# The MLP's down projection as seven block products: an fp32 decoder step on one Trainium2 core

## The chip, the cores and the metric

The kernel runs on one core of a Trainium2 chip. The metric is the device time of one execution in microseconds (us). TensorE is PE in the profile (its weight loads are PEld), VectorE is DVE, ScalarE is ACT, GpSimd is POOL and SyncE is SP. SP issues most of the transfers between HBM and SBUF here.

## The reference

The reference is one step of a two-layer decoder over 1056 tokens (1024 of a prompt and 32 of samples), width 1024, all in fp32. Each layer has a mixer (S5 and SSD scans in the first layer, sparse attention in the second) and then the MLP that this change is about:

```
D_MODEL = 1024;  D_FF = 4 * D_MODEL
rms_norm(x, g):  x * rsqrt(mean(x * x, -1) + 1e-5) * g
every layer:     x += relu(rms_norm(x) @ w_up)^2 @ w_down     # w_up 1024 x 4096, w_down 4096 x 1024
at the end:      y = rms_norm(x)
```

## The kernel before

**Three matmuls for a product.** TensorE takes its operands in the rounded fp32 form `fp32r`. To keep fp32's accuracy, each operand is split: hi is ACT's cast of it, lo is DVE's subtraction of hi from it. A product is hi·hi + hi·lo + lo·hi, three matmuls into the same PSUM bank (L384 to L386 in `dense`, L1355 to L1357 in the up projection). So every operand of TensorE costs one ACT and one DVE instruction first.

**The layout.** Activations lie with features on the 128 partitions and tokens along the free dimension. The 1056 tokens are two halves of `HF` = 528 in the MLP, each of two parts of 264.

**The up projection** (`mlp`, `prep`, `prod`) runs already as seven products of 2x2 blocks in place of eight: the weights and the normalised activations are each seen as 2x2 blocks, sums of blocks are formed, seven products p1 to p7 are made with matmuls of 264 columns, and the results are combined on the way out of PSUM (banks A, B and C). There are 16 passes `p`, each giving two of the 32 tiles of hidden features; the order of the products in a pass is p1, then p3 of the pass before, p6, p2, p7, p5, p4. `prep` makes the weights' sums on POOL (L1310) and splits them (L1321 and L1322). `act` makes relu² on DVE (L1337, a SCALAR_TENSOR_TENSOR), multiplies by `r2`, the squared norm factor of each token, on POOL (L1338), and SP writes the tile to the HBM buffer `h_d`.

**The down projection** (`h_load`, `down`, `dense`) is the plain product: 8 groups `G` of 512 hidden features x 8 output tiles `d` x 3 token chunks of 352 x 4 tiles `k` x 3 matmuls. For each group `h_load` reads four hidden tiles back from `h_d` and splits them (L330, L331); a unit of 512 KB of `w_dn` is loaded and split on ACT and DVE (L315, L316) with two buffers. DVE adds each finished bank into `Y` (L1400); at G = 6 the residual is added, at G = 7 `finish` squares `Y` and, after layer 0, makes the next layer's normalised operands `xn` (`resid`, L1192 and L1197).

**Order.** The program is written as one stream of Python; the tile framework gives every engine its own queue of instructions in program order, lifts work inside `tc.high_priority` (the weights' splits) ahead, and places the waits from tiles' buffers: a tile of a tag with n buffers waits until the nth tile before it was last read. `held` keeps the first two units of `w_dn` from being loaded before the up phase is nearly over. `W` carries the split activations of the up phase, `R` the raw weights, `SW` the split weights and `E` the partial results on their way out.

## Time and profile before

| | us |
|---|---|
| median of 3 runs | 3173.86 |
| lowest and highest | 3172.98, 3180.18 |
| the profiled execution | 3170.71 |
| its span in the trace | 3168.8 |
| PE busy | 3037.3 (96%) |
| DVE busy | 2081.9 (66%) |
| ACT busy | 1290.5 (41%) |
| POOL busy | 784.0 (25%) |

Busy times are those of instructions on an engine, and overlap with those of the others. The time outside the span (1.9 us in the profiled execution) is launch and end. A row of the timeline gives an instruction's start, its length and, in brackets, how long its engine was idle before and what released it; matmuls overlap in the array, so the distance from one start to the next, not the length, tells what a matmul costs.

### The profile page before, as it was taken

The numbers are of one execution on the slowest core, as the hardware profiler recorded it, in microseconds if no ns is written. First come the engines' busy times: TensorE is split into PE (matmuls) and PEld (weight loads), VectorE is DVE, ScalarE is ACT, GpSimd is POOL, SyncE is SP. The second block draws the span as 40 slices with busy tenths as digits, with TensorE's granted clock in tenths as the row PEclk, the third lists the DMA queues.
The fourth block names the chain that finished last, engine by engine and source line by source line (L and its number), as shares of the span: only waits on it lengthen the run. The fifth ranks groups of instructions, "written<-read, shape, count | busy, mean of one in ns | idle before, by whom it ended". The sixth has DMA issues, their size and how long they took to land. (4 is left out here: it accounts for less than half of the span.)

```text
span 3168.8 us, 55263 instructions
## 1 busy us (share of the span) xinstructions
PE 3037.3 (96%) x21451; PEld 2871.4 (91%) x21451; DVE 2081.9 (66%) x4075; ACT 1290.5 (41%) x2575; POOL 784.0 (25%) x771
## 2 busy tenths in 40 slices
PE   7999998998999999999999989999999999999998
PEld 5999886898999999999999777777778999999998
DVE  4778787788766444466224777878776776644456
ACT  4223666434333321123236666666653333331112
POOL 0000000016666200001001344343333666510000
PEclk8999999999999999999999999999999999999999
DMA  5345453522333532228631122121143233353232
GB/s 185 94 128 156 113 131 120 165 85 94 106 107 106 173 101 96 67 87 247 163 92 57 18 67 59 23 61 41 21 119 118 95 106 109 113 174 99 78 93 80
DMA packets 219852, 328.55 MB, mean 104 GB/s; under 512 B 71283, under 2 KB 164694, under 8 KB 219526
## 3 DMA queue, kind: packets, MB, share of 16 engines
q1 hardware_dynamic: 189760, 264.03, 27.5%
q0 software_dynamic: 17728, 36.77, 4.7%
q10 hardware_dynamic: 12102, 24.22, 2.0%
q8 instruction: 169, 2.77, 0.4%
q14 instruction: 93, 0.76, 0.1%
HBM read 224.30 MB, written 92.22 MB: 100 GB/s over the span
## 5 line engine op out<-in xcount | busy, mean ns | idle before, releaser
L384 PE MATMUL mm<-hh,wh 128*128 128x352 f32 x1440 | 465.1, 323 | 0.2 <-ACT c L1363 0.2
L386 PE MATMUL mm<-hh,wh 128*128 128x352 f32 x1440 | 464.9, 323 | 0.0
L385 PE MATMUL mm<-hh,wh 128*128 128x352 f32 x1440 | 464.5, 323 | 0.0
L1400 DVE TENSOR_TENSOR Y<-Y,mm 128x352 f32<-128x352 f32 x336 | 173.8, 519 | 273.1 <-PE mm L386 272.3
L315 ACT CAST wh<-wr 128x1024 fp32r<-128x1024 f32 (+3 forms) x121 | 122.9, 1016 | 468.8 <-PE mm L385 453.4
L1355 PE MATMUL A<-xw,sw 128*128 128x264 f32 x1024 | 291.7, 286 | 2.3 <-ACT xw L1215 1.6
L1357 PE MATMUL A<-xw,sw 128*128 128x264 f32 x1024 | 292.4, 286 | 1.0 <-DVE sw L1322 1.0
L1356 PE MATMUL A<-xw,sw 128*128 128x264 f32 x1024 | 293.0, 286 | 0.1
L2124 POOL TENSOR_SCALAR P<-P,s,gates 128x640 f32<-128x640 f32 (+7 forms) x256 | 211.9, 841 | 277.1 <-DVE s L2120 229.0
L385 PEld LDWEIGHTS mm<-hh,wh 128*128 128x128 f32 x1440 | 271.2, 188 | 0.0
L384 PEld LDWEIGHTS mm<-hh,wh 128*128 128x128 f32 x1440 | 270.7, 188 | 0.4 <-ACT c L1363 0.4
L386 PEld LDWEIGHTS mm<-hh,wh 128*128 128x128 f32 x1440 | 270.9, 188 | 0.0
L1338 POOL TENSOR_TENSOR e<-e,r 128x264 f32<-128x264 f32 x192 | 196.6, 1030 | 225.1 <-DVE e L1337 221.6
L384 PE MATMUL mm<-xh,wh 128*128 128x352 f32 x672 | 224.5, 335 | 7.0 <-ACT xh L435 5.9
L385 PE MATMUL mm<-xl,wh 128*128 128x352 f32 x672 | 222.5, 331 | 5.2 <-DVE xl L436 5.2
L386 PE MATMUL mm<-xh,wh 128*128 128x352 f32 x672 | 221.7, 330 | 0.0
L2142 DVE TENSOR_TENSOR PT<-px,PT 128x512 fp32r<-128x512 f32 x264 | 176.8, 682 | 51.2 <-ACT PT L2141 50.6
L316 DVE TENSOR_TENSOR wh<-wr,wh 128x1024 fp32r<-128x1024 f32 (+3 forms) x121 | 143.8, 1188 | 100.1 <-ACT wh L315 100.1
L2166 PE MATMUL pv<-PT,vs 128*128 128x512 f32 x528 | 195.3, 438 | 11.6 <-ACT PT L2141 6.8
L2116 ACT ACTIVATE P<-sc,m 128x640 f32<-128x640 f32 (+7 forms) x256 | 180.1, 713 | 41.0 <-DVE m L2110 30.1
L1355 PEld LDWEIGHTS A<-xw,sw 128*128 128x128 f32 x1024 | 193.8, 190 | 2.9 <-ACT xw L1215 1.7
L1357 PEld LDWEIGHTS A<-xw,sw 128*128 128x128 f32 x1024 | 194.1, 190 | 1.4 <-DVE sw L1322 1.4
(631 smaller groups left out, 8305.6 us busy)
## 6 DMA issues: line engine op xcount, KB each, us to landing
hr<-h_d SPq DMA_DIRECT2D x64, 528.0 KB
wu<-i_w_up SPq DMA_DIRECT2D x64, 512.0 KB
wr<-i_w_dn SPq DMA_DIRECT2D x64, 512.0 KB
h_d<-e SPq DMA_DIRECT2D x192, 132.0 KB
wr<-i_w_in_e POOLq DMA_DIRECT2D x26, 512.0 KB, 4.1
h_d<-c SPq DMA_DIRECT2D x64, 132.0 KB
res<-res SPq DMA_DIRECT2D x48, 176.0 KB
csb<-cs_d SPq DMA_DIRECT2D x16, 512.0 KB
```

The costliest lines, as they stand in the source:

```text
L384: T.matmul(o, wh, xh, start=(j == 0), stop=False)
L385: T.matmul(o, wh, xl, start=False, stop=False)
L386: T.matmul(o, wl, xh, start=False, stop=(j == n - 1))
L1338: nc.gpsimd.tensor_tensor(x, x, st["r2"][:, tok], OP.mult)
L1355: T.matmul(o, a, xh, start=bool(first and q == 0), stop=False, skip_group_check=True)
L1356: T.matmul(o, a, xl, start=False, stop=False, skip_group_check=True)
L1357: T.matmul(o, b, xh, start=False, stop=(q == 3), skip_group_check=True)
L1400: V.tensor_tensor(y[:, cc], y[:, cc], p[:, :CH], OP.add)
L2116: S.activation(P, reg[:, h - h0], AF.Exp, bias=b["m"][:, h:h + 1], accum_out=b["s"][:, h:h + 1])
L2124: nc.gpsimd.tensor_scalar(P, P, b["s"][:, h:h + 1], GT[:, qb, gc:gc + 1], op0=OP.mult, op1=OP.mult)
L2142: V.tensor_tensor(lo, p, hi.bitcast(F32), OP.subtract)
L2166: T.matmul(PV[g, qb, i], v, t, start=(a == 0 and kb == 0 and k == 0), stop=False)
```

## The change

The down projection becomes seven products of 2x2 blocks as well, taken in turn (p1, p5, p6, p7, p3, p2, p4). The blocks are halves of the hidden features within each pair of tiles, of the output tiles (`d` even and odd) and of the tokens. Each product runs 16 steps `q`; a step is 4 pairs of output tiles x 2 token parts x 3 matmuls of 264 columns into eight PSUM banks (`dn`) that the product keeps to its end. Each step reads its operands from HBM: 256 KB of weights (512 KB in p5) and 264 KB of activations, two steps ahead, and splits both on ACT and DVE (`two_of`). The weights' sums are made on DVE at the step (`ready`; p5 and p6 keep theirs in `SR`). The activations' sums t1 to t4 are made in the up phase by `t_sums`, four subtractions on DVE for each half of a pass, and written to HBM, so that a pass writes 14 tiles of 132 KB in place of 8. The multiplication by `r2` leaves the up phase (POOL, L1338) and is done once for each output in `scale_res` (DVE), which also loads the residual by a POOL transfer and adds it on POOL. In the last layer p4 runs in two halves of the tokens (`last`), with the final norm in four parts (`norm4`) between its steps. The tag `sw` has 2 buffers in place of 3, `e` has 12 in place of 9, and the start of the up phase prepares its operands in another order. The held units are now the first three of the next layer's input projection. In all, PE's queue grows from 18823 rows to 19593, DVE's from 3993 to 4526, ACT's from 2203 to 2575 and SP's from 932 to 1454, and POOL's shrinks from 696 to 576.

```diff
+        a[f"w_dn{l}"] = np.ascontiguousarray(wd.reshape(16, 2, 128, 4, 2, 128).transpose(4, 1, 0, 2, 3, 5).reshape(64, 128, 512))
...
+    def dn():
+        cnt[0] += 1
+        return psum[-1][1].tile([128, 512], F32, name=f"dn{cnt[0]}", tag="dn", bufs=8)
...
-    held = {U_MLP[l] + i for l in range(2) for i in range(2)}
+    held = {U_IO + i for i in range(3)}
...
+    h_d = [{n: dp.tile([16, 128, HF], F32, name=f"h{l}{n}_d") for n in ("b11", "b21", "b22", "t1", "t2", "t3", "t4")}
+           for l in range(2)]
...
-            t = wslot(F32R, "sw", "wh", 4) if i < 4 else ptile(F32R, "sw", "sw", 3, 1024)
+            t = wslot(F32R, "sw", "wh", 4) if i < 4 else ptile(F32R, "sw", "sw", 2, 1024)
...
-            return ptile(F32, "e", "e", 9, 264)
+            return ptile(F32, "e", "e", 12, 264)
...
+        def keep(n, p, c, x):
+            nc.sync.dma_start(h_d[l][n][p][:, c * 264:(c + 1) * 264], x)
+        def act(x, n, p, c):
             V.scalar_tensor_tensor(x, x, 0.0, x, op0=OP.max, op1=OP.mult)
-            nc.gpsimd.tensor_tensor(x, x, st["r2"][:, tok], OP.mult)
-            nc.sync.dma_start(h_d[l][f][:, tok], x)
+            E[p, c, n] = x
+            if n != "b12":
+                keep(n, p, c, x)
+        def t_sums(p, c):
+            b11, b12, b21, b22 = (E.pop((p, c, n)) for n in ("b11", "b12", "b21", "b22"))
+            t = xslot(F32, "ts")
+            t1, t2, t4 = (t[:, i * 264:(i + 1) * 264] for i in range(3))
+            for n, o, x, y in (("t1", t1, b12, b11), ("t3", b12, b22, b12), ("t2", t2, b22, t1), ("t4", t4, b21, t2)):
+                V.tensor_tensor(o, x, y, OP.subtract)
+                keep(n, p, c, o)
...
+                    t_sums(p, c)
...
+            if n == "p5":
+                prep(p, 6)
+            if p < 15 and n != "p3":
                 prep(p + 1, ORDER.index(wn))
...
+        def a_load(i, k, q):
+            t = half(F32, "ar")
+            nc.sync.dma_start(t, ins[f"w_dn{l}"][(2 * i + k) * 16 + q])
+            return t
+        BUF = ((lambda: ptile(F32, "br", "sw", 2, 1024)), (lambda: wslot(F32, "br", "w", 2)),
+               (lambda: ptile(F32, "br", "wr", 2, 1024)))
+        def b_load(n, q, o=0, m=HF):
+            cnt[0] += 1
+            t = BUF[q % 3]()
+            nc.sync.dma_start(t[:, :m], h_d[l][n][q][:, o:o + m])
+            return t[:, :m]
+        def two_of(x, t):
+            n = x.shape[-1]
+            hi, lo = t[:, :n], t[:, n:2 * n]
+            S.copy(hi, x)
+            V.tensor_tensor(lo, x, hi.bitcast(F32), OP.subtract)
+            return hi, lo
+        wt = lambda: wslot(F32R, "sb", "wh", 4)
+        xt_ = lambda: xslot(F32R, "xb")
+        XN = {p: x[1] for p, x in PROD.items()}
+        def ready(n, q):
+            if n == "p5":
+                a21, a22 = a_load(1, 0, q), a_load(1, 1, q)
+                if q % 2 == 0:
+                    SR["t"] = slot(F32, "st")
+                a = SR[q] = SR["t"][:, q % 2 * 512:(q % 2 + 1) * 512]
+                V.tensor_tensor(a, a21, a22, OP.add)
+            elif n in ("p6", "p7", "p3"):
+                w = a_load(*{"p6": (0, 0), "p7": (1, 1), "p3": (0, 1)}[n], q)
+                a = w if n == "p7" else SR[q]
+                V.tensor_tensor(a, *((SR[q], w) if n == "p6" else (w, SR[q])), OP.subtract)
+            else:
+                a = a_load(*{"p1": (0, 0), "p2": (0, 1), "p4": (1, 1)}[n], q)
+            x = b_load(XN[n], q)
+            return two_of(a, wt()), two_of(x, xt_())
...
+        def scale_res(d, cc):
+            y, res = Y[d][:, cc], half(F32, "res")[:, :264]
+            nc.gpsimd.dma_start(res, res_(d, cc))
+            V.tensor_tensor(y, y, st["r2"][:, cc], OP.mult)
+            nc.gpsimd.tensor_tensor(y, y, res, OP.add)
+        todo = []
+        def evac(n, dp, c, o):
+            d0, d1 = 2 * dp, 2 * dp + 1
+            if n in ("p1", "p5") and c == 0:
+                Y[d0 if n == "p1" else d1] = slot(F32, "Y")
+            y = lambda i, j: Y[d1 if i else d0][:, tok(j, c)]
+            if n == "p1":
+                S.copy(y(0, 0), o)
+            elif n == "p5":
+                S.copy(y(1, 1), o)
+            elif n == "p6":
+                V.tensor_tensor(y(1, 0), y(0, 0), o, OP.add)
+                nc.gpsimd.tensor_tensor(y(0, 1), y(1, 0), y(1, 1), OP.add)
+            elif n == "p7":
+                V.tensor_tensor(y(1, 1), y(0, 1), o, OP.add)
+                V.tensor_tensor(y(1, 0), y(1, 0), o, OP.add)
+                todo.append((d1, 1, c))
+            elif n == "p3":
+                V.tensor_tensor(y(0, 1), y(0, 1), o, OP.add)
+                todo.append((d0, 1, c))
+            elif n == "p2":
+                V.tensor_tensor(y(0, 0), y(0, 0), o, OP.add)
+                todo.append((d0, 0, c))
+                todo.append((d1, 0, c))
+            else:
+                t = e_t()
+                V.tensor_tensor(t, o, st["r2"][:, tok(0, c)], OP.mult)
+                V.tensor_tensor(y(1, 0), y(1, 0), t, OP.add)
+                finish(d1, tok(0, c), Y[d1])
+        def done(k):
+            d, j, c = k
+            scale_res(d, tok(j, c))
+            if (d % 2, j) != (1, 0):
+                finish(d, tok(j, c), Y[d])
...
+        def step(n, q, ops, cs=(0, 1)):
+            (wh, wl), (xh, xl) = ops
+            for dp in range(4):
+                a, b = (t[:, dp * 128:(dp + 1) * 128] for t in (wh, wl))
+                for c in cs:
+                    if q == 0:
+                        PS[dp, c] = dn()[:, :264]
+                    o = PS[dp, c]
+                    h, g = (t[:, c * 264:(c + 1) * 264] if len(cs) == 2 else t for t in (xh, xl))
+                    T.matmul(o, a, h, start=(q == 0), stop=False)
+                    T.matmul(o, a, g, start=False, stop=False)
+                    T.matmul(o, b, h, start=False, stop=(q == 15))
+                    if q == 15:
+                        evac(n, dp, c, o)
+        def down():
+            ks = [(n, q) for n in ("p1", "p5", "p6", "p7", "p3", "p2") + (() if l else ("p4",)) for q in range(16)]
+            ops = {}
+            for i, k in enumerate(ks):
+                if k == ("p5", 0):
+                    st["r2"] = bcast_tok(r, "r2", xslot(F32, "r2"))
+                for z in ([0, 1, 2] if i == 0 else [i + 2]):
+                    if z < len(ks):
+                        ops[z] = ready(*ks[z])
+                step(*k, ops.pop(i))
+                after(*k)
+                if k[0] in ("p3", "p2", "p4") and (k[1] % 2 or k[0] == "p4"):
+                    for _ in range(2 if k[0] == "p4" and k[1] < 4 else 1):
+                        if todo:
+                            done(todo.pop(0))
+        def last():
+            todo.sort(key=lambda k: (-k[1], k[2], k[0]))
+            for c in range(2):
+                ops = {}
+                for q in range(16):
+                    for z in ([0, 1, 2] if q == 0 else [q + 2]):
+                        if z < 16:
+                            x = b_load("t4", z, c * 264, 264)
+                            ops[z] = A22[z], two_of(x, wt())
+                    step("p4", q, ops.pop(q), (c,))
+                    for _ in range(2):
+                        if todo:
+                            done(todo.pop(0))
+                    hook(c, q)
...
         prep(0, 0)
-        prep(0, 1)
...
+            prep(0, {"t1": 4, "t3": 1, "t2": 3}[n])
         for q in range(4):
             b_split(W, "t4", q)
         W["a"].clear()
         prep(0, 5)
-        prep(0, 6)
+        V.reciprocal(r, r)
+        V.tensor_tensor(r, r, W["m1"], OP.mult)
         R[1] = up_raw(l, 1)
...
+        new_psum("dn")
+        down()
+        if l:
+            last()
```

DVE's queue around the end of layer 0's up phase, before. L1337 is relu², L1367 and L1375 the adds out of PSUM, L331 the split of a hidden tile and L316 that of a unit of `w_dn`, L1322 that of the up phase's weights:

```order
L1375 TENSOR_TENSOR e1393_10744<-e1393_10744,B1405_10840 128x264
L1337 SCALAR_TENSOR_TENSOR e1393_10744<-e1393_10744 128x264
L331 TENSOR_TENSOR hh1432_11133<-hr1430_11130,hh1431_11132 128x1056
L1322 TENSOR_TENSOR sw1414_10959<-sf1415_10960,sw1414_10959 128x512
L316 TENSOR_TENSOR wh1428_11125<-wr1426_11122,wh1427_11124 128x1024
L331 TENSOR_TENSOR hh1435_11139<-hr1433_11136,hh1434_11138 128x1056
L1367 TENSOR_TENSOR e1411_10910<-e1411_10910,C1418_10992 128x264
L1367 TENSOR_TENSOR e1413_10925<-e1413_10925,C1419_11009 128x264
```

After, at the same place: L1344 is relu², L1392 the add of p3, L1355 `t_sums`, L1427 the split in `two_of` (`sb` weights, `xb` activations, here the first steps of p1):

```order
L1344 SCALAR_TENSOR_TENSOR e1440_11087<-e1440_11087 128x264
L1427 TENSOR_TENSOR sb1457_11286<-ar1454_11282,sb1457_11286 128x512
L1355 TENSOR_TENSOR ts1452_11246<-e1440_11087,e1435_11012 128x264
L1392 TENSOR_TENSOR e1441_11101<-e1441_11101,B1447_11179 128x264
L1355 TENSOR_TENSOR e1440_11087<-e1444_11147,e1440_11087 128x264
L1355 TENSOR_TENSOR ts1452_11246<-e1444_11147,ts1452_11246 128x264
L1344 SCALAR_TENSOR_TENSOR e1441_11101<-e1441_11101 128x264
L1427 TENSOR_TENSOR sb1462_11296<-ar1459_11292,sb1462_11296 128x512
L1355 TENSOR_TENSOR ts1452_11246<-c211450_11212,ts1452_11246 128x264
L1355 TENSOR_TENSOR ts1453_11269<-e1441_11101,e1437_11027 128x264
L1427 TENSOR_TENSOR sb1467_11306<-ar1464_11302,sb1467_11306 128x512
L1427 TENSOR_TENSOR xb1458_11289<-br1456_11284,xb1458_11289 128x528
```

The splits of the first operands of the down projection (`hh`) stood ahead of the last products of the up phase; the first one of activations (`xb`) now stands behind the last `t_sums`.

DVE's queue in the middle of layer 0's down projection, before: one weights' split (L316) for every six adds out of PSUM (L1400):

```order
L316 TENSOR_TENSOR wh1665_12863<-wr1658_12789,wh1664_12862 128x1024
L1400 TENSOR_TENSOR Y1466_11319<-Y1466_11319,mm1663_12848 128x352
L1400 TENSOR_TENSOR Y1466_11319<-Y1466_11319,mm1666_12866 128x352
L1400 TENSOR_TENSOR Y1466_11319<-Y1466_11319,mm1668_12882 128x352
L1400 TENSOR_TENSOR Y1473_11368<-Y1473_11368,mm1669_12896 128x352
L1400 TENSOR_TENSOR Y1473_11368<-Y1473_11368,mm1670_12910 128x352
L1400 TENSOR_TENSOR Y1473_11368<-Y1473_11368,mm1671_12924 128x352
L316 TENSOR_TENSOR wh1674_12953<-wr1667_12879,wh1673_12952 128x1024
```

After, at the change from p7 to p3: L1481 and L1482 are p7's two adds for a bank, L1463 is the multiplication by `r2` in `scale_res`:

```order
L1427 TENSOR_TENSOR sb1853_13626<-st1544_11790,sb1853_13626 128x512
L1427 TENSOR_TENSOR xb1854_13629<-br1852_13624,xb1854_13629 128x528
L1481 TENSOR_TENSOR Y1675_12471<-Y1555_11840,dn1772_13099 128x264
L1482 TENSOR_TENSOR Y1675_12471<-Y1675_12471,dn1772_13099 128x264
L1427 TENSOR_TENSOR sb1858_13677<-st1568_11893,sb1858_13677 128x512
L1481 TENSOR_TENSOR Y1675_12471<-Y1555_11840,dn1773_13103 128x264
L1482 TENSOR_TENSOR Y1675_12471<-Y1675_12471,dn1773_13103 128x264
L1463 TENSOR_TENSOR Y1675_12471<-Y1675_12471,r21559_11873 128x264
L1481 TENSOR_TENSOR Y1676_12480<-Y1556_11849,dn1774_13107 128x264
```

Steps are two splits each (L1427), and the adds for the eight banks of a product come together at its end, with splits for later steps between them.

DVE's queue at the end of layer 0's down projection, before. L1197 makes lo of the next operands, L1192 adds squares, L316 splits the next layer's first units (`wx`):

```order
L1192 TENSOR_TENSOR acc2969_7013<-acc2969_7013,sq1878_14410 128x352
L1197 SCALAR_TENSOR_TENSOR xn1840_14095<-Y1484_11460,p_norm_mix_odd_7011,xn1839_14094 128x352
L1197 SCALAR_TENSOR_TENSOR xn1845_14118<-Y1488_11503,p_norm_mix_odd_7011,xn1844_14117 128x352
L1400 TENSOR_TENSOR Y1495_11552<-Y1495_11552,mm1881_14436 128x352
L1691 MEMSET vbd_14484 128x512
L1197 SCALAR_TENSOR_TENSOR xn1845_14118<-Y1488_11503,p_norm_mix_odd_7011,xn1844_14117 128x352
L1197 SCALAR_TENSOR_TENSOR xn1851_14143<-Y1495_11552,p_norm_mix_odd_7011,xn1850_14142 128x352 x2
L316 TENSOR_TENSOR wx1909_14644<-wr1896_14516,wx1908_14643 128x1024
```

After: L1493 and L1494 are p4's multiplication by `r2` and add into `Y`, L1191 and L1200 belong to `resid`, L313 splits the next layer's second unit (`wh2209`):

```order
L1494 TENSOR_TENSOR Y1675_12471<-Y1675_12471,e2177_15597 128x264
L1493 TENSOR_TENSOR e2181_15621<-dn2084_14996,r21559_11873 128x264
L1494 TENSOR_TENSOR Y1675_12471<-Y1675_12471,e2179_15609 128x264
L1493 TENSOR_TENSOR e2183_15633<-dn2085_15000,r21559_11873 128x264
L1493 TENSOR_TENSOR e2185_15645<-dn2086_15004,r21559_11873 128x264
L1494 TENSOR_TENSOR Y1676_12480<-Y1676_12480,e2181_15621 128x264
L1191 TENSOR_TENSOR acc2969_7025<-acc2969_7025,sq2178_15600 128x264
L1493 TENSOR_TENSOR e2187_15657<-dn2087_15008,r21559_11873 128x264
L1493 TENSOR_TENSOR e2189_15669<-dn2088_15012,r21559_11873 128x264
L1200 SCALAR_TENSOR_TENSOR xn1875_13756<-Y1675_12471,p_norm_mix_odd_7023,xn1874_13755 128x264
L1494 TENSOR_TENSOR Y1676_12480<-Y1676_12480,e2183_15633 128x264
L313 TENSOR_TENSOR wh2209_15755<-wr2207_15752,wh2208_15754 128x1024
```

The split of the unit, which stood among the finishing work of the last output tile, now stands behind seven of p4's multiplications (two of them ahead of these rows), four of its adds and two instructions of the finishing work.

## Rows read from the trace of the kernel before

**Rows 1.** Windows by stage: start and end, length, then the columns named.

```profile
core 0: us, PE busy (x) PEld busy (x) DVE busy (x) ACT busy (x) POOL busy (x), PEclk, DMA share, GB/s
900.00:1000.00 100.00, 100.00 (x824) 100.00 (x823) 69.94 (x103) 34.52 (x74) 66.38 (x59) 1.00 0.34 106
1200.00:1300.00 100.00, 100.00 (x627) 100.00 (x626) 47.15 (x70) 18.91 (x19) 0.00 (x0) 1.00 0.27 87
```

**Rows 2.** PE's timeline at the ends of the two down phases: start, length, instruction.

```profile
1066.36 0.32 PE L384 MATMUL mm<-hh,wh 128*128 128x352 f32 x1
...
1440.26 0.38 PE L1543 MATMUL mm<-wh,xn 128*128 128x256 f32 x1 [0.47 <-DVE xn L1197]
...
2783.14 0.32 PE L384 MATMUL mm<-hh,wh 128*128 128x352 f32 x1
...
3156.20 0.32 PE L386 MATMUL mm<-hh,wx 128*128 128x352 f32 x1
```

**Rows 3.** PE's timeline: first and last of 52, then of 40, matmuls in sequence.

```profile
899.76 0.28 PE L1355 MATMUL A<-xw,sw 128*128 128x264 f32 x1
...
905.98 0.28 PE L1355 MATMUL A<-xw,sw 128*128 128x264 f32 x1
...
1199.72 0.33 PE L385 MATMUL mm<-hh,wh 128*128 128x352 f32 x1
...
1205.99 0.32 PE L385 MATMUL mm<-hh,wh 128*128 128x352 f32 x1
```

**Rows 4.** Groups by line: busy us, mean ns of one, idle before and releaser.

```profile
L1322 DVE TENSOR_TENSOR sw<-sf,sw 128x512 fp32r<-128x512 f32 x128 | 112.8, 883 | 89.0 <-ACT sw L1321 88.8
L1337 DVE SCALAR_TENSOR_TENSOR e<-e 128x264 f32<-128x264 f32 x192 | 119.4, 623 | 6.0
L1371 DVE TENSOR_TENSOR e<-e,B 128x264 f32<-128x264 f32 x64 | 27.2, 425 | 13.2 <-PE B L1357 12.8 <-ACT e L1360 0.2
L1338 POOL TENSOR_TENSOR e<-e,r 128x264 f32<-128x264 f32 x192 | 196.6, 1030 | 225.1 <-DVE e L1337 221.6 <-issue 3.2 <-DMA wu<-i_w_up 0.4
```

**Rows 5.** DVE's and POOL's timelines in the up phase.

```profile
901.46 1.48 POOL L1310 TENSOR_TENSOR sf<-wu 128x512 f32<-128x512 f32 x1
...
901.71 1.77 DVE L1322 TENSOR_TENSOR sw<-wu,sw 128x512 fp32r<-128x512 f32 x1
...
912.48 0.69 DVE L1322 TENSOR_TENSOR sw<-wu,sw 128x512 fp32r<-128x512 f32 x1
```

**Rows 6.** PE's waits: waiting line, releaser, us in all, times, longest.

```profile
PE C L1357 <- DVE sw L1322: 12.2, 2, 6.1
...
PE A L1355 <- ACT e L1360: 0.7, 2, 0.5
```

**Rows 7.** Windows at layer 0's up start, columns as in rows 1.

```profile
725.00:800.00 75.00, 66.97 (x510) 65.84 (x511) 64.84 (x90) 33.96 (x72) 52.04 (x40) 0.93 0.26 87
735.00:740.00 5.00, 1.23 (x5) 1.23 (x6) 5.00 (x4) 1.71 (x4) 5.00 (x4) 0.59 0.39 111
740.00:745.00 5.00, 4.62 (x28) 4.41 (x27) 5.00 (x5) 0.00 (x0) 3.34 (x2) 0.72 0.25 98
```

**Rows 8.** DMA of 1440 to 1500 in 40 slices: busy tenths, GB/s.

```profile
DMA  9999999999899998996898999995889608700000
GB/s 265 309 348 413 419 422 416 415 377 244 281 283 323 337 227 304 322 262 132 182 151 313 403 361 272 274 334 122 131 308 343 259 0 153 284 0 0 0 0 0
```

**Rows 9.** Timeline after layer 0's down phase: last DVE finish, first ACT evacuation.

```profile
1445.03 0.51 DVE L1192 TENSOR_TENSOR acc<-acc,sq 128x352 f32<-128x352 f32 x1
...
1450.27 0.47 ACT L1628 ACTIVATE q<-mm,rq 128x256 f32<-128x256 f32 x1 [0.37 <-DVE rq L1503]
```

**Rows 10.** DVE's timeline after the last product of the program.

```profile
3157.08 1.77 DVE L2336 TENSOR_TENSOR acc<-acc,sq 128x352 f32<-128x352 f32 x3
...
3161.72 1.57 DVE L2360 SCALAR_TENSOR_TENSOR Y<-Y,p_norm_final,px 128x352 f32<-128x352 f32 x3 [1.06 <-PE px L2357]
```

More of the change, by code (lines that the diff above doesn't have):

```diff
@@ L1182, in _build, with sq_add, resid @@
     g_mlp = param("norm_mlp")
-    def resid(d, c, src, g, xn, acc):
-        cc = slice(c * CH, (c + 1) * CH)
-        if d == 0:
+    seen = set()
+    def sq_add(acc, cc, src, key):
+        if (key, cc.start) not in seen:
+            seen.add((key, cc.start))
             S.activation(acc[:, cc], src, AF.Square)
         else:
-            t = half(F32, "sq")[:, :CH]
+            t = half(F32, "sq")[:, :cc.stop - cc.start]
             S.activation(t, src, AF.Square)
             V.tensor_tensor(acc[:, cc], acc[:, cc], t, OP.add)
-        if c == 0:
+    def resid(d, cc, src, g, xn, acc):
+        sq_add(acc, cc, src, "acc2")
+        if d not in xn:
             xn[d] = slot(F32R, "xn"), slot(F32R, "xn")
@@ new lines, in after @@
+        def after(n, q):
+            if n == "p2" and l:
+                A22[q] = two_of(a_load(1, 1, q), slot(F32R, "a22"))
+        tok = lambda j, c: slice((1 - j) * HF + c * 264, (1 - j) * HF + (c + 1) * 264)
+        res_ = lambda d, cc: res_d[2 * l][d][:, cc]
+        def scale_res(d, cc):
[3 more added lines that the diff above has]
+            nc.gpsimd.tensor_tensor(y, y, res, OP.add)
@@ L1418, in mlp @@
         prep(0, 0)
-        prep(0, 1)
-        for n in ("b11", "b21"):
-            for q in (2, 3):
-                b_split(W, n, q, xslot if n == "b11" or q == 2 else slot)
+        sums(0, "s2")
+        for q in (2, 3):
+            b_split(W, "b11", q, xslot)
+        for q in (2, 3):
+            b_split(W, "b21", q, xslot if q == 2 else slot)
         prep(0, 2)
-        prep(0, 4)
         for q in (2, 3):
@@ L2325, in _build, with fin4, norm4 @@
     YF = {}
-    acc4 = slot(F32, "acc4")
-    def fin4(d, c, y):
+    def fin4(d, cc, y):
+        if not YF:
+            YF["acc"] = slot(F32, "acc4")
         YF[d] = y
-        cc = slice(c * CH, (c + 1) * CH)
-        if d == 0:
-            S.activation(acc4[:, cc], y[:, cc], AF.Square)
-        else:
-            t = half(F32, "sq")[:, :CH]
-            S.activation(t, y[:, cc], AF.Square)
-            V.tensor_tensor(acc4[:, cc], acc4[:, cc], t, OP.add)
-        for k, at in enumerate(((2, 1), (2, 2), (7, 2))):
-            if at == (d, c):
-                norm4(k)
-    r4 = const("rf", [128, 9])
-    def norm4(c):
+        sq_add(YF["acc"], cc, y[:, cc], "acc4")
+    r4 = const("rf", [128, 12])
+    V.memset(r4, 1.0)
+    def norm4(t):
         p = px()
-        n = [min(128, CH - i * 128) for i in range(3)]
+        o, n = t * 264, (128, 128, 8)
         for i in range(3):
-            o = c * CH + i * 128
-            T.matmul(p[:n[i], i:i + 1], acc4[:, o:o + n[i]], C["ones"][:, 0:1], start=True, stop=True)
-        r = r4[:, 3 * c:3 * c + 3]
-        V.memset(r, 1.0)
+            T.matmul(p[:n[i], i:i + 1], YF["acc"][:, o + i * 128:o + i * 128 + n[i]], C["ones"][:, 0:1], start=True, stop=True)
+        r = r4[:, 3 * t:3 * t + 3]
         V.tensor_scalar(r[:, :2], p[:, :2], 1.0 / D, EPS, op0=OP.mult, op1=OP.add)
```

128 lines of the change are left out of this document (35 added, 93 removed).

## The prediction, made before the changed kernel ran

> **What bounds the kernel now.** I read the windows by stage first. In the middle of an up phase and of a down phase PE is busy for all of 100 us at full clock, while DVE is busy for 69.94 and 47.15 us and the DMA engines for a third of their time [rows 1]. So in both stages the number of PE's columns sets the time, and what is left out of PE's work is won unless something else becomes late. The timeline gives the stages' ends: layer 0's down phase runs from 1066.36 to 1440.26, 373.9 us, layer 1's from 2783.14 to 3156.20, 373.1 us [rows 2]. The cadence, from one start to the next, says what a matmul costs: 51 steps in 6.22 us are 0.1220 us for 264 columns, 39 steps in 6.27 us are 0.1608 us for 352 [rows 3]. Per column they agree within 1.5%, so shorter matmuls lose nothing. The waits of PE come last: the longest in the MLP is 6.1 us, once in each layer's up start [rows 6].
>
> **Columns.** Down now issues 8 x 8 x 3 x 4 x 3 = 2304 matmuls of 352, 2304 x 0.1608 = 370.5 us. After it issues 7 x 16 x 4 x 2 x 3 = 2688 of 264, 2688 x 0.1220 = 327.9. That is -42.6 a layer and -85.2 for both. A step of 24 matmuls lasts 2.93 us; every operand has to come, be split and be read within that.
>
> **From up to down.** Before, the first operands were split ahead of the last products, and the phases join without a gap. Now the first activations' lo stands on DVE behind the last `t_sums`. After the up phase's last matmul DVE still has an add, a relu², five subtractions of 264 (0.425 alone [rows 4]) and three splits of about 0.69 [rows 5]. Seven of 0.35 to 0.43 and 2.1 are 4.6 to 5.1 us, less about 1 us of hi·hi matmuls that PE can do meanwhile: about 3.8. A stall has a price beyond itself: at layer 0's up start PE waits 6.1 us [rows 6], the granted clock then is 0.59 and 0.72 [rows 7], nearer the 1.2 than the 2.4 GHz level, and in 740 to 745 PE does 28 matmuls where 5 / 0.122 = 41 fit, 1.6 us lost, with some 0.6 before it: 8.3 for 6.1. So 3.8 costs about 5 a layer, 10 in all; bounds 0 (other queues empty sooner) and 18 (the wait is 6.1 and more, since the load of that operand waits for a buffer of `sw` that p4 of the last pass holds).
>
> **VectorE in the steps.** p1, p2 and p4 have two splits a step, 2 x 0.69 = 1.4 us of 2.93. p5, p6, p7 and p3 have a sum more, 2.1. With p3 come p7's adds (16 of 0.43, 6.9 us) and, in layer 0, eight finishing pieces of three instructions of 264 (1.3 each, 10.4): 16 x 2.07 + 6.9 + 10.4 = 50.4 against 16 x 2.93 = 46.9. In layer 1 a finishing piece has two, and the sum is 46.9. POOL's adds of the residual fall there too, and a DVE instruction that meets POOL's is longer: 1.77 in place of 0.69 [rows 5]. I take +3, for p3 of layer 0 alone; bounds 0 and 3.5 + 8 x 1.08 = 12 for each layer, if each of the eight POOL adds lengthens one.
> The Trainium skill bears on this, page "SBUF — State Buffer", section "SBUF: two separate sides": VectorE with two SBUF inputs and GpSimd share a pair of ports that is locked for a whole instruction, not divided. The trace agrees: the instruction of 901.71 ends 0.54 after POOL's. By that rule alone the sum would move to the upper of the two bounds, +24 in place of +3.
>
> **Other changes of product.** All eight banks end together, but PE's queue has the next product's first steps bank by bank behind the adds. The nearest row is the up phase's wait of a bank for its copy, 0.7 in two waits [rows 6]. Six changes a layer, 0.25 each: +3 for both; bounds 0 and 16 (a DVE queue of eight adds, 3.4 us, seen by PE at a third of them).
>
> **End of layer 0.** In before, DVE's last finishing work ends at 1445.54 and the first bank of the next projection leaves at 1450.27 [rows 9], 4.7 us for the norm's factor, under 4 banks x 24 matmuls x 0.122 = 11.7 us of PE. Now p4's eight banks ask for four DVE instructions each at the very end (multiply, add, square's sum, lo; about 1.7), 13.9 us, while PE makes them in 2.9: DVE ends 11 us after PE, and 11 + 4.7 - 11.7 = 4 us are open. The split of the next layer's second unit stands behind thirteen of these instructions, 2 to 3 us more of which part is the same time. With the clock +7; bounds 0 and 16.
>
> **Tail.** Before, the last group of DVE's adds of squares starts at 3157.08 and the last normalising multiplications at 3161.72 [rows 10]. Now the last part has 264 tokens in place of 352, but p4's two DVE instructions more and a matmul chain between steps: +2; bounds -2 and +6.
>
> **Up phase.** Start: 75 - 510 x 0.122 = 12.8 us are lost in 725 to 800 [rows 7]; the new order asks POOL for the second sum sooner and splits fewer weights ahead of the activations. I take -2 a layer, -4; bounds -12 and +4. Steady state: a pass is 168 matmuls, 20.5 us. DVE gets 8 x 0.43 = 3.4 us more, 14.3 + 3.4 = 17.7 of 20.5. POOL loses 8 x 1.03 = 8.2 us [rows 4], which shortens DVE's collisions: relu² takes 0.62 on average, 0.43 where nothing collides, so 1.5 of the 3.4 come back on these alone. Hidden while DVE stays under 20.5: 0; bounds -2 and the third rival's price.
>
> **Transfers.** Down asks for 256 + 264 KB a step, 532,480 bytes in 2.93 us, 182 GB/s; p5 for 271. Up writes 14 x 132 KB a pass in place of 8, 40 GB/s on top of 106 [rows 1]. After the down phase of layer 0 the core moved 413 to 422 GB/s in five slices of 1.5 us, but also 122 to 182 in slices just as busy [rows 8]. SP has 522 instructions more in all (1454 in place of 932), spread over 650 us and more. Cost 0, hidden by two steps' lead (5.9 us); without that lead every step shows its own load.
>
> **Sum.** -85.2 + 10 + 3 + 3 + 7 + 2 - 4 = -64. On the profiled 3170.7 (its span of 3168.8 and 1.9 around it) that is 3106.5; the median of the runs shown stands 3.2 above the profiled one, so 3109. The terms' bounds, with errors that partly cancel, give 3085 to 3138.
>
> **Rivals.**
> *VectorE becomes the bound.* For it: 50.4 against 46.9 in p3, 1.77 for an instruction that collides. Against it: POOL loses all its work in the up phase and has only about 40 adds in a down phase. If 3 instructions a step went at 0.883 each, the mean of the up phase [rows 4], with p7's adds and the pieces, p5 to p3 would be some 12 to 20 us late in a layer; 45 in all with the transitions' upper bound gives 3109 + 45 = 3154.
> *The up phase pays.* Each half pass's sums lie in a tile that is free again only when its writes have landed, and DVE's queue stands still until then: adds, relu² and the weights' splits behind it. At 1.5 us a pass over 32 passes, 48 us, 3157. Against it: 17.7 of 20.5 leaves 2.8 a pass, which is eaten first.
> *Transfers become the bound, and it is slower.* In the down phases, 16 x (6 x 532,480 + 794,624) bytes are 63.8 MB. Divided by the present 373.9 us that is 171 GB/s: below this rate the down phase is longer than before. At 150, between the slow slices and that rate [rows 8], it takes 425 us, 51 more for each layer: 3174 + 103 = 3277. For it: the busy slices of 122 to 182. Against it: those belong to a stretch with gathers, and 87 GB/s at a share of 0.27 and 106 at 0.34 [rows 1] are over 310 at a full share, in stages with transfers of 512 and 528 KB, twice the new ones.
> The Trainium skill speaks for this rival, page "DMA: Bandwidth & Descriptors", section "Measured (HBM→SBUF, 128 partitions, SWDGE, issued from GpSimd)": it wants transfers of 1 MiB or more for three quarters of the peak, and lists 138 GB/s at 64 KB and 341 at 1 MB. An estimate from that page for 256 KB is 2.0 us, 132 GB/s, if they went one by one; by it a down phase would take 483 us. The trace disagrees as far as it goes, with 322 GB/s at full share for loads of 512 and 528 KB.
> *It doesn't do what it says:* shorter matmuls that cost as much as long ones, 2688 x 0.1608 = 432, 3174 + 117 = 3291. The cadence of the up phase speaks against it [rows 3].
>
> **Chances.** Forecast (3085 to 3138) 0.69; VectorE 0.12; up phase 0.08; transfers 0.07, the last 0.01; 0.03 for something better than all the bounds. The two middle rivals spread about their prices, and a quarter of them ends within 0.3% or above. A measurement of this kernel can tell about 0.3% from no change, 3164 to 3183: faster 0.86, same 0.05, slower 0.09. The range for 8 in 10 goes from 3085 to 3162; the likeliest's own is 3085 to 3138.
>
> **What would show it.** Columns: a cadence of 0.122 in both down phases and a down phase of 335 to 350 us from its first matmul to the next stage's. From up to down: one PE wait of 3 to 5 us for an `xb` split on DVE, with a lower clock for the next 5 us. VectorE: PE's waits for DVE in p3 of layer 0 and none in p2. End of layer 0: a PE idle of about 5 us in the first 20 us of the next projection. Transfers: a DMA share under 0.7 in p1, under 0.95 in p5, and no PE or DVE wait put down to a load. Wrong would be: PE busy under 95% in the middle of a down or up phase, or a down phase over 360 us.

## The result and the profile after

The changed kernel takes 3134.16 us (median of 4 executions, 3129.79 to 3135.01) where the kernel before takes 3173.83 (3172.98 to 3180.18): ratio 0.9868, 95% interval 0.9851 to 0.9885. Timed again beside other kernels it took 3131.11. The forecast was 3109, a gain of 65; the gain is 40. The profiled execution took 3129.79, its span 3128.0.

The stages of both kernels in two profiles each, from the start of a stage's first matmul to the start of its last, as PE's timeline gives them. Mixer 0 runs from its first projection's matmul to the up phase. The up phase is cut after its first 400 matmul records; this first part is called the up start below. "Join" is from the start of the up phase's last matmul to the first of down. Mixer 1 runs from down's last matmul to the next up phase, so it holds the end of layer 0. The tail runs from the last matmul of layer 1's down phase to the end of the span.

| us | mixer 0 | up, first 400 (L0, L1) | up, rest | join | down | mixer 1 | tail |
|---|---|---|---|---|---|---|---|
| before | 699.6 | 62.2, 61.8 | 278.6, 279.3 | 0.1, 0.1 | 370.7, 373.1 | 1004.8 | 12.7 |
| before again | 705.6 | 62.2, 61.9 | 278.6, 279.3 | 0.1, 0.1 | 370.8, 373.1 | 1000.9 | 12.6 |
| changed | 706.7 | 66.2, 66.2 | 278.6, 278.3 | 7.1, 3.9 | 335.3, 336.3 | 1012.3 | 13.6 |
| changed again | 706.9 | 66.2, 66.1 | 278.6, 278.3 | 6.4, 5.1 | 336.9, 336.6 | 1009.0 | 13.2 |

Windows of the changed kernel, columns as in [rows 1]: the join of layer 0, then p5, p6, p3 and p4.

```profile
1078.00:1082.00 4.00, 0.00 (x0) 0.00 (x0) 2.36 (x6) 1.60 (x3) 0.00 (x0) 0.68 0.98 291
1082.00:1086.00 4.00, 3.78 (x17) 3.78 (x18) 3.85 (x8) 1.76 (x4) 0.00 (x0) 0.50 1.07 339
1132.00:1178.00 46.00, 46.00 (x380) 46.00 (x379) 40.60 (x66) 20.81 (x40) 0.00 (x0) 1.00 0.93 324
1180.00:1225.00 45.00, 45.00 (x371) 45.00 (x370) 21.98 (x35) 17.86 (x31) 1.14 (x2) 1.00 0.37 102
1274.00:1318.00 44.00, 42.65 (x348) 42.22 (x348) 38.60 (x77) 21.32 (x44) 16.79 (x13) 1.00 0.64 199
1370.00:1410.00 40.00, 37.56 (x308) 37.35 (x308) 28.43 (x49) 20.18 (x40) 17.01 (x24) 1.00 0.78 254
```

In p5 and p6 PE is as full as in [rows 1]; in p5 the transfers run at 0.93 of their time and 324 GB/s, and PE does not wait for one. Around and in the down phase PE loses at three places: the join (no matmul in 4 us, then 17 at a granted clock of 0.50, the lower level), p3 and p4. The waits of PE in the changed kernel, in the form of [rows 6], say for what:

```profile
PE dn L1513 <- ACT xb L1426: 10.5, 2, 6.8
...
PE A L1372 <- ACT sw L1326: 8.5, 2, 4.8
PE A L1372 <- ACT xw L1232: 5.1, 2, 2.7
...
PE dn L1514 <- DVE xb L1427: 2.6, 4, 1.1
...
PE dn L1513 <- ACT sb L1426: 2.4, 1, 2.4
PE px L1904 <- DMA gb<-ga: 2.4, 2, 1.9
```

The first is the join: both times for ACT's cast of the first activations, and not for DVE. The next two are the up starts. The two `dn` rows behind them are p3 (1.09 and 0.26 in layer 0, 0.69 in layer 1; 0.52 more is in p1 of layer 1) and p4 of layer 0. The last row is in layer 1's mixer, behind layer 0's down phase: PE transposes blocks gathered from the attention's cache (`gb`) and waits for their loads.

PE's timeline at the ends of the stages answers to [rows 2]:

```profile
1082.22 1.03 PE L1513 MATMUL dn<-xb,sb 128*128 128x264 f32 x3 [6.83 <-ACT xb L1426]
...
1418.94 0.36 PE L1660 MATMUL mm<-wh,xn 128*128 128x256 f32 x1 [1.15 <-DVE e L1493]
...
2778.17 0.39 PE L1513 MATMUL dn<-xb,sb 128*128 128x264 f32 x1 [3.63 <-ACT xb L1426]
...
3114.45 0.29 PE L1515 MATMUL dn<-sb,a 128*128 128x264 f32 x1
```

From 1082.22 to 1418.94 are 336.7 us, against 373.9 before. Behind layer 0's down phase the next stage is not late at once. Its 114th matmul starts 17.1 and 17.0 us after the down phase's last one in the two profiles of the changed kernel, against 16.2 and 15.5 before; its 127th starts at 22.3 and 23.1, against 17.7 and 17.0. Between these two stand twelve of the transposes of `gb`; the kernel before has its first ones only after 190 matmuls, and none waits there.

### The profile page after: what moved, and what is told of

Its sections match the earlier page's. It is cut to its first block, busy times and chain, and to the rows that moved or that the text cites. A ratio compares the mean times of both kernels' runs of the same rounds, so it can differ in the third digit from the quotient of the medians.

```text
span 3128.0 us, 58908 instructions
## 1 busy us (share of the span) xinstructions
PE 2970.6 (95%) x22228; PEld 2798.3 (89%) x22228; DVE 2204.7 (70%) x4618; ACT 1412.5 (45%) x2920; POOL 662.9 (21%) x659
## 5 line engine op out<-in xcount | busy, mean ns | idle before, releaser
L1514 PE MATMUL dn<-xb,sb 128*128 128x264 f32 x1664 | 473.0, 287 | 2.6 <-DVE xb L1427 2.6
L1515 PE MATMUL dn<-xb,sb 128*128 128x264 f32 x1664 | 468.2, 285 | 0.0
L1513 PE MATMUL dn<-xb,sb 128*128 128x264 f32 x1664 | 455.3, 286 | 12.9 <-ACT xb L1426 10.5
L1513 PEld LDWEIGHTS dn<-xb,sb 128*128 128x128 f32 x1664 | 306.8, 189 | 13.5 <-ACT xb L1426 10.9
L1514 PEld LDWEIGHTS dn<-xb,sb 128*128 128x128 f32 x1664 | 315.1, 189 | 3.5 <-DVE xb L1427 3.4
L1515 PEld LDWEIGHTS dn<-xb,sb 128*128 128x128 f32 x1664 | 316.0, 190 | 0.0
L1372 PEld LDWEIGHTS A<-xw,sw 128*128 128x128 f32 x1024 | 195.6, 192 | 17.5 <-ACT sw L1326 9.0
L1373 PEld LDWEIGHTS A<-xw,sw 128*128 128x128 f32 x1024 | 195.4, 191 | 4.1 <-DVE xw L1233 4.1
L2260 ACT CAST PT<-px 128x512 fp32r<-128x512 f32 x264 | 152.6, 594 | 98.3 <-PE px L2271 97.3
L1374 PEld LDWEIGHTS A<-xw,sw 128*128 128x128 f32 x1024 | 196.1, 192 | 0.0
L2215 PE MATMUL sc<-KT,qt 128*128 128x256 f32 x1216 | 193.6, 298 | 0.0
L2229 DVE TENSOR_REDUCE m<-sc 128x1 f32<-128x640 f32 (+7 forms) x176 | 167.0, 949 | 30.9 <-PE sc L2215 26.9
```

The costliest lines, as they stand in the source:

```text
L1372: T.matmul(o, a, xh, start=bool(first and q == 0), stop=False, skip_group_check=True)
L1373: T.matmul(o, a, xl, start=False, stop=False, skip_group_check=True)
L1374: T.matmul(o, b, xh, start=False, stop=(q == 3), skip_group_check=True)
L1513: T.matmul(o, a, h, start=(q == 0), stop=False)
L1514: T.matmul(o, a, g, start=False, stop=False)
L1515: T.matmul(o, b, h, start=False, stop=(q == 15))
```

## The experiments

**The join.** The theory after the result came from ACT's timeline at the join of the changed kernel:

```profile
1075.59 0.62 ACT L1426 CAST sb<-ar 128x512 fp32r<-128x512 f32 x1 [2.70 <-DMA ar<-i_w_dn]
1078.47 0.62 ACT L1426 CAST sb<-ar 128x512 fp32r<-128x512 f32 x1 [2.26 <-DMA ar<-i_w_dn]
1081.02 0.62 ACT L1426 CAST sb<-ar 128x512 fp32r<-128x512 f32 x1 [1.93 <-DMA ar<-i_w_dn]
1081.54 1.70 ACT L1426 CAST xb<-br 128x528 fp32r<-128x528 f32 x3
```

The weights of three steps are cast first, each when its load lands, 2.5 to 2.9 us apart; the first activations come fourth. DVE's queue has the same order (`sb1467` ahead of `xb1458` in the rows of the change). The edit issues the first three steps inside the last pass:

```diff
-        BUF = ((lambda: ptile(F32, "br", "sw", 2, 1024)), (lambda: wslot(F32, "br", "w", 2)),
-               (lambda: ptile(F32, "br", "wr", 2, 1024)))
+        BUF = ((lambda: wslot(F32, "br", "w", 2)), (lambda: ptile(F32, "br", "wr", 2, 1024)),
+               (lambda: ptile(F32, "br", "sw", 2, 1024)))
...
                 prod(*((p, n) if n else (p - 1, "p3")))
+                if p == 15 and n == "p1":
+                    for q in range(4):
+                        del W["x"]["b11", q]
+                if p == 15 and n in ("p2", "p7", "p4"):
+                    z = ("p2", "p7", "p4").index(n)
+                    pre[z] = ready("p1", z)
```

> The changed kernel, with the loads and splits of p1's first three steps issued inside the last pass of the up phase (after its p2, p7 and p4), activations' loads into buffers that are free then. In the changed kernel PE idles 6.8 us (layer 0) and 3.6 + 0.5 us (layer 1) between the phases, and the clock is at 0.78 and 0.66 for the next 10 us. Theory (ACT casts the weights of three steps, whose loads land 2.7 us apart, before the first activations): both gaps go and the clock with them, 11 us of idle and some 5 of clock less, minus what the last products lose to splits, so 3134 - 13 = 3121. Rival of the prediction (lo stands on DVE behind the last sums of activations): the splits are ahead of these now too, so the gap goes as well, but the wait that remains would be for DVE and 1 to 2 us. Rival (the last up writes and the first loads compete for the DMA engines): gap 3 to 5 us stays, 3128 to 3131.

Measured: 3121.77 us (3118.87 to 3123.88), 0.9835 (0.9818 to 0.9851); joins of 0.1 and 0.1 us. What is left is a wait of the third matmul bank for the up phase's last adds:

```profile
1078.27 0.39 PE L1513 MATMUL dn<-xb,sb 128*128 128x264 f32 x1 [1.74 <-DVE e L1392]
```

So the join came from when the first operands are ready, and to mend it is worth 9 to 12 us. p1 stays 2.8 and 2.1 us longer than p6 (49.7 and 49.0 us), now at the full clock, with the wait above and one of 0.99 us in layer 1. The edit moves loads and casts at once, and the order alone was not tried. The trace of the changed kernel has the landing, though: the load of the first activations is issued at 1072.80, and the semaphore that their cast waits for has its last signal at 1076.91. The cast at 1081.54 comes 4.6 us later, behind that of the third step's weights, which landed at 1080.99. So in layer 0 it is the order on ACT, and not the landing, that holds the first activations for these 4.6 us, while PE stands for 6.8.

**The up start.** It was to gain 2 us a layer and lost 4. First the order alone:

```diff
         prep(0, 0)
-        sums(0, "s2")
...
+        prep(0, 1)
+        for n in ("b11", "b21"):
...
```

> The changed kernel, with the start of the up phase prepared in the order of the kernel before (both weights' sums first, then the splits of b11 and b21, the prep of s1 ahead of the sums of activations); prep of s4 stays at p5. The two up starts of the changed kernel idle PE for 4.8 + 2.4 + 0.9 + 1.9 us (layer 0) and 3.8 + 2.8 + 2.3 + 0.8 us (layer 1), where the kernel before idles 6.1 + 1.2 and 6.1 + 1.0. Theory (the new order itself costs: POOL's sums of activations come late because DVE's splits run back to back and POOL gets through none of its work, one POOL sum took 9.95 us): the idles and low clock of the kernel before come back, about 4 us less a layer, 3134 - 8 = 3126. Rival (the start is longer because `sw` has a buffer fewer or through something in the steady state): within 2 us of 3134. If the reordering were worth the 2 us a layer that the prediction gave it: 3138.

Measured: 3131.28 us (3128.97 to 3131.98), 0.9865 (0.9849 to 0.9882), up starts of 65.6 and 67.0. The theory fell. Then the token halves as before, with the old order:

```diff
-        return W["a"][2 * q + k][:, (1 - j) * HF:(2 - j) * HF]
+        return W["a"][2 * q + k][:, j * HF:(j + 1) * HF]
...
-        tok = lambda j, c: slice((1 - j) * HF + c * 264, (1 - j) * HF + (c + 1) * 264)
+        tok = lambda j, c: slice(j * HF + c * 264, j * HF + (c + 1) * 264)
...
```

> The changed kernel with the token halves taken as before (block 0 is the first 528 tokens) and with the old order at the up start; the final norm's parts are taken in the order in which they then come. With the old order alone (the run before) the up starts stayed at 65.6 and 67.0 us. Theory (the swapped halves make the first operands b11 depend on the last chunk of tokens, so all eight of their splits stand behind the last residual add, and POOL's sums behind these): the up starts go back to 62 to 63 us, 3.5 us less a layer; against it layer 0's next projection waits longer for its first tokens, which now come last, 2 to 5 us more. In all 3134 - 7 + 4 = 3131. Rival (a third `sw` buffer, that is s4 prepared at the start, is what the old start had): up starts stay at 65 to 67.

Measured: 3127.35 us (3121.81 to 3130.78), 0.9852 (0.9834 to 0.9871), up starts of 67.3 and 66.5. This fell too. The median is 4 to 7 us below the changed kernel's, which nothing here explains: the execution that was profiled is the slowest of the four, 3130.78 us, though its mixer 0, which no edit touched, was short (701.2). Then, on the kernel before, the later preparation of s4:

```diff
-            t = wslot(F32R, "sw", "wh", 4) if i < 4 else ptile(F32R, "sw", "sw", 3, 1024)
+            t = wslot(F32R, "sw", "wh", 4) if i < 4 else ptile(F32R, "sw", "sw", 2, 1024)
...
-        prep(0, 6)
...
+            if n == "p5":
+                prep(p, 6)
```

> The kernel before with one part of the change in the up phase alone: two `sw` buffers in place of three, so that s4 of a pass is prepared after its p5 and not with the pass before (at the start: not ahead of the first products). In the changed kernel the first 400 records of PE in an up phase take 66.2 us against 62.2 and 61.9 before; neither the old order there (65.6, 67.0) nor the old halves with it (67.3, 66.5) changed that. Theory (the later s4 is what is left of the difference): 65 to 67 us here too, 3173 + 8 = 3181. Rival (POOL's first sum for pass 1, which in the changed kernel is released 3 to 6 us later, at a moment when DVE leaves it no gap, and holds up the sums of activations behind it): 61 to 63 us here, if the sum is not held up here, 3171 to 3175.

Measured: 3176.64 us (3173.15 to 3179.69), 1.0011 (1.0001 to 1.0021), up starts of 62.2 and 61.1, but 280.0 and 280.5 for the rest of the phase. The third buffer is not the cause there either. What the slow up starts have in common is on POOL, where one sum of 1.3 to 1.8 us takes far longer (10.26 and 9.04 us in layer 0 of the first two runs). POOL's timeline in the changed kernel, layer 0:

```profile
732.19 9.95 POOL L1315 TENSOR_TENSOR sf<-wu 128x512 f32<-128x512 f32 x1 [7.01 <-DMA wu<-i_w_up]
742.10 1.29 POOL L1242 TENSOR_TENSOR xa<-xa,xa 128x528 f32<-128x528 f32 x1
```

DVE's timeline at that time, and then ACT's:

```profile
738.47 2.55 DVE L1233 TENSOR_TENSOR xw<-xa,xw 128x528 fp32r<-128x528 f32 x4
744.09 1.09 DVE L1233 TENSOR_TENSOR xw<-xa,xw 128x528 fp32r<-128x528 f32 x1 [3.08 <-ACT xw L1232]
```

```profile
743.42 0.63 ACT L1232 CAST xw<-xa 128x528 fp32r<-128x528 f32 x1 [5.56 <-POOL xa L1242]
```

POOL's first sum for the next pass of weights takes 9.95 us where [rows 5] show 1.48, while DVE runs one instruction after the other (no idle in its timeline from 729.6 to 741.0); it ends 1.1 us after DVE stops at 741.0. The sums of activations stand behind it on POOL, ACT's casts behind these, and DVE and PE then wait. In the kernel before, POOL took turns with DVE at the same place:

```profile
729.65 1.70 POOL L1225 TENSOR_TENSOR xa<-xa,xa 128x528 f32<-128x528 f32 x1 [2.58 <-DVE xa L1225]
731.32 1.74 POOL L1310 TENSOR_TENSOR sf<-sf,wu 128x512 f32<-128x512 f32 x1
```

```profile
730.10 1.82 DVE L1225 TENSOR_TENSOR xa<-xa 128x528 f32<-128x528 f32 x1
731.85 1.78 DVE L1216 TENSOR_TENSOR xw<-xa,xw 128x528 fp32r<-128x528 f32 x1
```

The next edit takes the sums of activations off POOL:

```diff
-                    b_sum(W, q, ("t3", "t2", "t4"))
+                    b_sum(W, q, ("t3", "t2", "t4"), V)
```

> The changed kernel, with the six sums of activations of the up start that POOL makes for q = 2 and 3 made by DVE. Theory (at the up start POOL's instructions are held up by DVE's: one POOL sum of 7.2 us, one of 9.95): the sums cost DVE 6 x 0.69 = 4.1 us but come when they are asked for; the PE idles of 4.8 + 2.4 us and 3.8 + 2.8 us shrink to about half, up starts of 62 to 64 us, 3134 - 5 = 3129. Rival (DVE's own work is the bound of the up start): it gets longer by 2 to 4 us a layer, 3134 + 6 = 3140.

Measured: 3116.76 us (3116.56 to 3116.78), 0.9825 (0.9808 to 0.9841), up starts of 62.2 and 60.5. POOL's sum is held up as before, for 11.70 us now, and nothing waits for it:

```profile
733.09 11.70 POOL L1315 TENSOR_TENSOR sf<-wu 128x512 f32<-128x512 f32 x1 [7.13 <-DMA wu<-i_w_up]
```

The same edit on the kernel before:

> The kernel before with the up start's six sums of activations on DVE in place of POOL. Theory (in the kernel before POOL's sums took turns with DVE's instructions, 1.7 us each, and were not held up for long, so this is a cost of the new order): the up starts of 62.2 and 61.9 us stay within 1.5 us, 3173 +- 3. Rival (the sums on POOL were too late in the kernel before as well, so that what the last run won has nothing to do with the change): up starts of 58 us, 3165.

Measured: 3165.41 us (3159.26 to 3168.75), 0.9975 (0.9966 to 0.9985), up starts of 57.7 and 57.7. So the rival holds: POOL's sums cost the kernel before 4 us a layer as well, and the changed kernel's up start is still 3 to 4.5 us longer when both have them on DVE. That the sums on POOL cost 4 to 6 us a layer, in either kernel, is shown; what the change adds on top is not, and POOL's held-up sum does not explain it. The order and the halves (tried on the changed kernel) and the third buffer (tried on the kernel before) are not it. PE's timelines say where it sits. The first matmul comes 0.1 us after the norm's last one in the changed kernel and 1.0 and 0.9 us before, so 0.9 us a layer is a matter of where the stage is cut. After 96 matmuls the changed kernel is not behind (24.0 against 24.2 us in layer 0, 22.9 against 24.3 in layer 1); the next 48, the products p7 and p4 of the first pass, take 10.8 and 11.6 us in place of 6.8 and 6.3.

**VectorE and the transfers**, the rivals of the prediction. Without the weights' sums:

```diff
-                V.tensor_tensor(a, a21, a22, OP.add)
+                a = a21
...
-                a = w if n == "p7" else SR[q]
-                V.tensor_tensor(a, *((SR[q], w) if n == "p6" else (w, SR[q])), OP.subtract)
+                a = a_load(*{"p6": (0, 0), "p7": (1, 1), "p3": (0, 1)}[n], q)
```

> The changed kernel without the sums of weights in the down phase: p5, p6, p7 and p3 use one raw block of weights in place of a sum (it leaves out 4 x 16 DVE instructions a layer; all loads stay). Theory (VectorE is hidden but for p3, where PE waits 1.09 + 0.26 + 0.69 us for it): 1 to 3 us less, 3131 to 3133. Rival of the prediction (VectorE bounds the steps with three DVE instructions): 20 us less and more, 3114 or below.

Measured: 3123.25 us (3120.33 to 3132.21), 0.9846 (0.9826 to 0.9866). The time looks like a middle between the two, but the stages say that the sums cost nothing: down takes 334.6 and 337.1 us, within 2.3 us of the changed kernel's two profiles. The rest lies in mixer 0 (703.4), the join (5.8) and mixer 1 (1009.6), where nothing was edited and where profiles differ by as much. In p3 of layer 0 PE waits 1.09 us at its 105th matmul with the sums and without them. In the changed kernel the split that it waits for stands on DVE behind thirteen multiplications by `r2`:

```profile
1279.80 3.52 DVE L1463 TENSOR_TENSOR Y<-Y,r 128x264 f32<-128x264 f32 x10
...
1284.15 1.11 DVE L1463 TENSOR_TENSOR Y<-Y,r 128x264 f32<-128x264 f32 x3
...
1285.79 0.69 DVE L1427 TENSOR_TENSOR xb<-br,xb 128x528 fp32r<-128x528 f32 x1
```

With one more load a step:

```diff
             x = b_load(XN[n], q)
+            a_load(0, 0, q)
```

> The changed kernel with one more load of 256 KB in every step of the down phase, which nothing reads. A step then brings 794,624 bytes in 2.93 us, 271 GB/s (as p5 did, without a wait of PE), and p5 1,056,768, 361 GB/s. Theory (transfers are hidden with room to spare): p5 alone becomes bound by transfers, at some 320 GB/s 3.3 us a step, 16 x 0.37 = 6 us a layer, and the start of the phase about 1 us more: 3134 + 14 = 3148. Rival (a transfer of 256 KB costs a time of its own, so the kernel is already near its bound): 3134 + 60 and more, since every step would be late.

Measured: 3163.45 us (3156.62 to 3174.53), 0.9963 (0.9951 to 0.9975). Both were off. The loss is 30 us, between the two, and not in p5:

```profile
1132.00:1178.00 46.00, 46.00 (x380) 46.00 (x379) 31.84 (x51) 20.75 (x40) 0.00 (x0) 1.00 0.97 342
1370.00:1410.00 40.00, 29.77 (x215) 28.72 (x214) 25.87 (x44) 15.58 (x30) 17.72 (x25) 0.93 0.89 289
```

p5 moves 342 GB/s and PE stays full. p4 of layer 0 takes 70.0 us in place of 49.5, and p7, from its first matmul to the first of the next product, 50.6 and 52.2 in place of 47.0 and 46.9. In p4 the next stage's loads and the residuals run beside the steps.

**What differs from execution to execution.** Layer 0's mixer has the same instructions on PE in both kernels:

> The kernel before, unchanged, profiled once more. In its first profile layer 0's mixer, the same instructions in the same order on PE as in the changed kernel, takes 699.6 us from its first projection's matmul to the up phase; the changed kernel and the three variants that ran so far took 703.4 to 708.9. If the change does something to that stretch (memory that lies elsewhere, a queue): 699 to 701 again. If the stretch simply differs from execution to execution: somewhere in 700 to 709.

Measured: 3171.04 us (one execution), mixer 0 in 705.6. Over the profiles it takes 699.6 to 708.9, so this stretch is no part of the change.

> The changed kernel, unchanged, timed beside the next two. 3134 +- 3 by its first four times. Its up starts (first 400 records of PE) 66.2 and 66.2 us, against 62.2 and 61.8 before; the joins of the phases 7.1 and 3.9 us as in its first profile if they are a matter of order, otherwise different.

Measured: 3131.11 us (3129.75 to 3133.29), 0.9872 (0.9856 to 0.9889); its stages are in the table.

**Both edits together**, the early first steps and the sums on DVE:

> The changed kernel with both edits that paid: the first three steps' loads and splits inside the last pass of the up phase, and the up start's six sums of activations on DVE. Apart they gave 3121.8 (the joins 7.1 and 3.9 us to 0.1) and 3116.8 (the up starts 66.2 and 66.2 us to 62.2 and 60.5) from 3131 to 3134. Theory (two places that have nothing to do with each other): the gains add, 3132 - 11 - 15 = 3106, joins of 0.1 us, up starts of 61 to 62 us. Rival (what one saves the other had saved too, for example through the clock): 3112 and more.

Measured: 3109.78 us (3105.03 to 3112.30), 0.9804 (0.9790 to 0.9818): faster than both kernels. Joins 0.1 and 0.1, up starts 62.4 and 60.5, so both stages keep what they had won apart. The median lies between the forecast of 3106 and the rival's 3112, and the executions cover both; in the time the gains add within this spread.

Then a longer lead of the loads:

```diff
-                for z in ([0, 1, 2] if i == 0 else [i + 2]):
+                for z in ([0, 1, 2, 3] if i == 0 else [i + 3]):
```

> The run before with operands three steps ahead in the down phase in place of two. What is left there is 1.8 us over in p3 (PE waits for the splits that stand behind p7's adds) and 2.6 us in p4 of layer 0 (a load of weights lands late, with the next stage's loads beside it). Theory (the lead of two steps, 5.9 us, is what runs out at both): both shrink to under 0.5, 3106 - 4 = 3102. Rival (a buffer, not the lead, holds the loads: weights' splits have four buffers, which three steps ahead fill up): no change, 3106 +- 1, or PE waits for splits in other steps, 3108 to 3115.

Measured: 3110.63 us (3104.48 to 3113.78), 0.9804 (0.9790 to 0.9818). p4 of layer 0 goes from 51.5 to 47.4 us, so its late load was a matter of lead; p3 stays at 49.0 with a wait of 1.08 us for the same split, so its wait is DVE's queue. Both are read from one profile of each kernel. In the time no gain is seen.

## Why the prediction was right in the whole and wrong at the up start

- *Columns, -85*: right. p2, p5 and p6 take 46.8 to 46.9 us each, 384 x 0.1220.
- *From up to down, +10*: the place was right, the cause wrong, the size too small. PE waited not for DVE behind `t_sums` but for ACT, which cast three steps' weights ahead of the first activations. The two joins hold 11.0 us of idle, and p1 takes 2.8 and 4.6 us more than p6 (with 0.5 of later wait), most of it at the lower clock. DVE's printed rows have the same order, three `sb` ahead of `xb`; the prediction counted them as 2.1 us of work and not as waits for three loads, and it did not read ACT's order.
- *VectorE, +3 in p3*: right in place; the size came out by luck. p3 takes 48.7 us in layer 0 and 47.8 in layer 1, 1.8 and 0.9 over p6. But the sum of DVE's work, 50.4 against 46.9, is not what PE lost: without the weights' sums p3 has 11 us of this work less (16 x 0.69), and in layer 0 the same wait. It is the order on DVE, one split behind thirteen multiplications. The down phase is no shorter without the sums, so VectorE's rival is refuted.
- *Other changes of product, +3*: nothing; p5 and p6 begin without a wait.
- *End of layer 0, +7*: the size came, by another way than predicted, so this is luck too. Mixer 1 is 7.8 us longer on the mean of two profiles each. DVE's finishing work does end late, 11.8 us after PE's last matmul where 11 was forecast, but PE never stands for the norm's factor. It waits 1.15 us for a bank and 0.34 for the second unit's split, and at the 114th matmul it is only 1.2 us later than before. It loses 3.7 and 4.6 us at the twelve transposes behind that one, with waits of 2.4 and 3.2 us for loads of `gb`, which the prediction does not have; why they come earlier in PE's order is open. p4's 2.6 us over p6 come on top: a weights' load that landed late, where the prediction had put transfers at nothing.
- *Tail, +2*: 0.8 by the table, and 2.9 more in p4 of layer 1 (4.5 in the second profile), with the norm's matmuls in it. So it is somewhat too small and within its bounds.
- *Up start, -4*: this step failed, with its sign, and outside its bounds of -12 and +4. It is +8: 66.2 twice, against 62.2 and 61.8, in [rows 7]'s stage (some 6.7 when counted from the norm's last matmul). The argument was that POOL gets its second sum sooner and that fewer weights are split ahead of the activations. What the runs show is that p7 and p4 of the first pass take 4.0 and 5.3 us longer. The argument also left out that POOL's sums stand in one queue behind a sum that can be held up while DVE runs, but these sums cost the kernel before as much, so the cause of the +8 stays open. It is the largest miss, 12 of 25 us.
- *Steady state, 0*: right, 278.6 before and after in layer 0, with fourteen writes a pass in place of eight; the up phase's rival is refuted.
- *Transfers, 0*: right to 2.6 us. The Trainium skill's rule of 1 MiB (page "DMA: Bandwidth & Descriptors", section "Measured (HBM→SBUF, 128 partitions, SWDGE, issued from GpSimd)") does not bind here: loads of 256 and 264 KB, many at a time on SP's queue, moved 324 GB/s in p5.

The 25 us between 65 and 40 are then: up starts 12, joins with p1 8, p4 of layer 0 about 3, the tail with p4 of layer 1 about 2, less the 3 of the product changes that did not come; the rest is within what mixer 0 does by itself. The columns carry the result, and the time lies in the forecast's range, near its upper end; two of the smaller terms, p3 and the end of layer 0, are right in number alone.

## What to carry to other kernels

A cut in matmul columns arrives in full where PE was full; what it loses is at the seams. At a seam, read the order of every engine ahead of the first matmul, ACT's too, and count every instruction that stands ahead of the first operands with the wait for its own load. The rows suggest to put the first step's operands whole before the second step's; that alone was not tried. Where a start shares work between VectorE and GpSimd, give its term wide bounds on both sides of nothing: the order of the instructions does not tell which engine is held up.
